# Banded heads of a hybrid attention layer: probabilities turned by DMA transposes instead of TensorE

## The chip, the cores and the metric

The kernel runs on one core of one Trainium2 chip. The metric is the device time of one execution in microseconds. The program has one launch; three runs of the kernel before gave 1187.77, 1191.12 and 1192.73 us, a median of 1191.12.

## What is computed

One decoder layer over 2048 positions of width 1024 (batch 1). A pre-normalised input goes through one projection that feeds two groups of eight heads of 64: the Fox heads (causal attention over all positions with a forget-gate bias) and the banded heads (a sliding window of 128 with a learned sink per head, four query heads to a key head). Each group's output is gated, both go through one output projection, are normalised and added to the input. The change is in the banded heads:

```python
def sliding_window_sink_attention(q, k, v, sinks):
    B, S, _, d = q.shape
    nb = S // Q_BLOCK
    ...
    kk, vv = with_prev(k), with_prev(v)
    s = jnp.einsum('bnqhgd,bnshd->bnhgqs', qb, kk, preferred_element_type=jnp.float32) * (d ** -0.5)
    ...
    band = (rel >= 0) & (rel < WINDOW)
    ...
    s = jnp.where(mask[None, :, None, None], s, -jnp.inf)
    ...
    p = jax.nn.softmax(jnp.concatenate([s, sink], axis=-1), axis=-1)[..., :-1]
    out = jnp.einsum('bnhgqs,bnshd->bnqhgd', p.astype(vv.dtype), vv)
    return out.reshape(B, S, SWA_Q_HEADS * d)
```

A block of 128 queries sees its own block of keys and the one before; the softmax has the sink as one more column.

## The kernel before

**Stages.** The kernel runs its stages one after the other: the start (adaLN, normalised input turned into `hT`), a prologue of projections, the banded stage (about 146 to 431 us of the profile), the Fox stage, and the output projection. Numbers are carried as a high and a low part in fp16, so that a product takes three matmuls (high times high, high times low, low times high).

**Order.** The order within each engine is written out by hand. Projection work is cut into units (3 matmuls of 512 columns, or 12 of 128) in a list `punits`; `fill(n)` issues the next n units, with the weight events that hang on them. `after(n, f)` queues f for the n-th next `tick()`, which is how evacuations of projection results follow some time behind their matmuls. Three PSUM banks `bk` (five in the Fox stage) take the results of projections; an evacuation releases its bank.

**The banded stage.** It works through 32 pairs (`Pair`): a pair is two query heads `j` of one key head and two blocks `i`, `i+1` of 128 queries. That is four score blocks of 128 x 256, or, for the first pair of each `j`, two of 128 x 128 and two of 128 x 256. So a pair has eight blocks of 128 x 128 probabilities (`nt`), and four of the pairs have six. One turn of the loop (L1100) is called a period here. In period n, PE's projection units are issued in four parts with a tick ahead of each, and around them stand:

- `maxima` of pair n (L855): DVE reads the scores from PSUM, adds the band mask, writes them to the tile `sm_` in SBUF, and takes row maxima (L865). POOL puts the sink into the column behind them (L863). One DVE operation makes the four negated maxima `nb` (L869).
- `exps` of pair n after the first part (L871): ACT takes the exponential in place, four operations, with the row sums.
- at the end of the period, `pv` of pair n-1 (L897): PE multiplies the turned probabilities `ptt` with the values (L904); at the next tick DVE scales the result (L910) and POOL sends it to DRAM (L912).
- then `turn` of pair n (L878): PE transposes the f32 probabilities of `sm_` block by block into the PSUM tile `pxb` (L885). At the next tick ACT copies them to fp16 as the high part (L894), and at the tick after that DVE subtracts to get the low part (L890), both into `ptt`. DVE also takes the reciprocal of the row sums there.
- then `scores` of pair n+1 (L844): PE, into the PSUM tile `pss`, of which there is one.
- last, ACT's squares of a piece of the output weights (L1123), and SP's load of the next piece (L1127).

PSUM in this stage: three banks `bk`, two for `pss`, two for `pxb`, one for `pob` (the result of `pv`). Rotated queries come in chunks of 512 positions (`evac_rope`): ACT copies the projection out, SP swaps its halves by four DMAs (L712), DVE forms sine and cosine terms six ticks later, and two ticks after that the chunk's low part is done (L719); the chunk is a tile of the pool `abp` with four buffers. The pool `stp` with two buffers of 2 KB per partition holds the same for the keys, in the prologue only.

**Queues.** SP, POOL and ACT issue DMAs in program order, each waiting where its instruction waits. In the banded stage SP has the four swaps per chunk and one weight load per period; POOL has the weights of later projections, the round trips of their maxima through DRAM (`w_max`, `w_back`), the sink copies and the results.

**Start of the Fox stage.** `key_limbs(hd)` (L1213) makes three limbs of a head's gate sums on DVE, six small operations into the tile `lk`; `key_rows(hd)` (L1225) turns them by a PE matmul (L1199) and has them copied out and sent to the head's tile. Head 1 needs both ahead of the first score step (L1522 to L1525), behind a loop that issues units, maxima of the first head and ticks.

Of the kernel before, what the change touches and what calls it, by code (L numbers as in the profile page):

```python
# [10 lines left out]
F32 = mybir.dt.float32  # L11
F16 = mybir.dt.float16
# [6 lines left out]
P = 128  # L19
# [22 lines left out]
def hybrid_layer(  # L42
# [38 lines left out]
    def sm(n, tag):  # L81
        return small.tile([P, n], F32, tag=tag, name=tag)
# [110 lines left out]
    def after(n, f):  # L193
        late.append([n, f])
# [460 lines left out]
    def open_fox():  # L655
        nonlocal abp
        xlx.close()
        abp = swa_pool("abp", 4)
        early.close()
        fxv = right.enter_context(tc.tile_pool(name="fxv", bufs=1, side="right", reuse_waits="tile"))  # L660
        vt = fx["vt"] = fxv.tile([P, NB, 8, VW], F16, name="vt")
        fx["lk"] = fxv.tile([P, LW], F16, name="lk")
        fx["lq"] = [fxv.tile([P, LW], F16, name=f"lq{n}") for n in range(2)]
        fx["cst"] = cst = fxv.tile([P, XR], F16, name="cst")
        fx["crow"] = fxv.tile([P, P], F16, name="crow")
        for ap, val in ((vt[:, :, :, 64:65], 1.0), (cst[:], 0.0), (fx["lk"][:], 0.0), (fx["lq"][0][:], 0.0),
                        (fx["lq"][1][:], 0.0), (cst[:, 64:65], XA), (cst[:, 65:66], XB),
                        (cst[:, 66:67], XA), (cst[:, 67:68], XB), (cst[:, 68:69], XC)):
            V.memset(ap, val)
# [15 lines left out]
    def swa_pool(name, bufs, **kw):  # L685
        return swa.enter_context(tc.tile_pool(name=name, bufs=bufs, reuse_waits="tile", **kw))
# [147 lines left out]
    class Pair:  # L834
# [20 lines left out]
        def maxima(self):  # L855
            key = f"qb{self.j}"
            snk2 = snk[:, 2 * self.j:2 * self.j + 2]

            self.sm_ = sws.tile([P, 2, 2, 2 * P + 1], F32, tag="ss", name="sm_")
            m = sm(4, "b_m")  # L860
            for e, (i, k0, nk) in enumerate(self.blocks):
                w = nk * P
                G.tensor_copy(self.sm_[:, e, :, w:w + 1], snk2.unsqueeze(2))  # L863
                for h in range(2):
                    V.tensor_tensor_reduce(self.sm_[:, e, h, :w], self.pss[:, h, e * 2 * P:e * 2 * P + w],  # L865
                                           bmask[:, 2 * P - w:], scale=scl[key][:], scalar=snk2[:, h:h + 1],
                                           op0=ALU.add, op1=ALU.max, accum_out=m[:, 2 * e + h:2 * e + h + 1])
            self.nb = sm(4, "b_nb")
            V.tensor_scalar(self.nb[:], m[:], -1.0, LIFT, op0=ALU.mult, op1=ALU.add)  # L869

        def exps(self):  # L871
            self.rs = sm(4, "b_rs")
            for e, (i, k0, nk) in enumerate(self.blocks):
                for h in range(2):
                    p, c = self.sm_[:, e, h, :nk * P + 1], slice(2 * e + h, 2 * e + h + 1)
                    A.activation(p, p, AF.Exp, bias=self.nb[:, c], accum_out=self.rs[:, c])

        def turn(self):  # L878

            nt = self.nt  # L880
            px = ps_t.tile([P, 8, P], F32, tag="t", name="pxb")
            for e, (i, k0, nk) in enumerate(self.blocks):
                for h in range(2):
                    for b in range(nk):
                        PE.transpose(px[:, self.at[e] + h * nk + b, :], self.sm_[:, e, h, b * P:(b + 1) * P], ident[:])  # L885
            self.ptt = ptp.tile([P, 2, 8, P], F16, tag="pt", name="ptb")
            hi, lo = self.ptt[:, 0, 0:nt, :], self.ptt[:, 1, 0:nt, :]

            def low():
                V.tensor_tensor(lo, px[:, 0:nt, :], hi, op=ALU.subtract)  # L890
                self.rinv = sm(4, "b_ri")
                V.reciprocal(self.rinv[:], self.rs[:])

            after(1, lambda: A.activation(hi, px[:, 0:nt, :], AF.Copy))  # L894
            after(2, low)

        def pv(self):  # L897
            j, i = self.j, self.i
# [183 lines left out]
    with swa_order:  # L1082
        fill(N_PRO - 4, tick2)
        psx.close()
        sws = swa_pool("sws", 1)
        ptp = swa_pool("ptp", 1)
        ps_s = swa_pool("ps_s", 1, space=PSUM)
        ps_t = swa_pool("ps_t", 1, space=PSUM)
        ps_pv = swa_pool("ps_pv", 1, space=PSUM)
        wsp = swa_pool("wsp", 2)  # L1090
        wss, wst = sm(16, "a_m"), sm(2, "wst")
        wsq = {}
        base = N_PRO
        NW = len(windows)
        windows[0].scores()
        windows[0].maxima()
        fill(2, tick2)
        windows[0].exps()
        fill(2, tick2)
        for n, wd in enumerate(windows):  # L1100
            goal = base + (N_SWA - base) * (n + 1) // NW
            todo = goal - pos[0]
            part = [todo * (m + 1) // 4 - todo * m // 4 for m in range(4)]
            tick()
            if n:
                wd.maxima()
            fill(part[0])
            tick()
            if n:
                wd.exps()  # L1110
            fill(part[1])
            tick()
            fill(part[2])
            tick()
            fill(part[3])
            if n:
                windows[n - 1].pv()
            wd.turn()
            if n + 1 < NW:
                windows[n + 1].scores()  # L1120

            if n:
                A.activation(wsq[n - 1][:], wsq[n - 1][:], AF.Square, accum_out=wss[:, (n - 1) % 16:(n - 1) % 16 + 1])  # L1123
            if n == 16:
                V.tensor_reduce(wst[:, 0:1], wss[:], axis=AX.X, op=ALU.add)
            wsq[n] = wsp.tile([P, 2 * P], F32, tag="wsq", name="wsq")
            SP.dma_start(wsq[n][:], w_out0[n // 4 * P:(n // 4 + 1) * P, n % 4 * 2 * P:(n % 4 + 1) * 2 * P])  # L1127
        tick()
        fill(5)
        tick()  # L1130
        fill(5)
        tick()
        fill(6)
        windows[NW - 1].pv()
        tick()
        tick()
        A.activation(wsq[NW - 1][:], wsq[NW - 1][:], AF.Square, accum_out=wss[:, 15:16])
        V.tensor_reduce(wst[:, 1:2], wss[:], axis=AX.X, op=ALU.add)
        wsum = sm(1, "w_mx2")
        V.tensor_reduce(wsum[:], wst[:], axis=AX.X, op=ALU.add)  # L1140
# [363 lines left out]
    with tc.manual_schedule():  # L1504
# [8 lines left out]
        pw_ = bk[bank()][:, 0:1]  # L1513
        PE.matmul(pw_, ones[:], wsum[:], start=True, stop=True)
        root_scale(wrt[:], pw_)
        while pos[0] < N_V3 or mi < M_LEAD:
            fill(1)
            if mi < M_LEAD and pos[0] >= N_QK0 - 12:
                munits[mi]()
                mi += 1  # L1520
            tick()
        key_limbs(1)  # L1522
        for _ in range(3):
            tick()
        key_rows(1)  # L1525
# [113 lines left out]
```

## Time and profile before

| | |
|---|---|
| Median of three runs | 1191.12 us |
| Profiled execution: its time, its span | 1192.12 us, 1190.1 us |
| PE, DVE, ACT busy in the span | 96%, 77%, 56% |
| Granted TensorE clock, mean | 0.994 |
| Pairs of the banded stage, blocks turned | 32, of which 28 with eight blocks and 4 with six |

The profile is one execution. A row of a group gives line, engine and operation, out<-in with shapes and count, then busy time and mean ns of one, then the idle time of the engine ahead of them and what ended it. A row of the timeline gives the start in us, the duration, the instruction, and in brackets the idle time before it with its releaser. A row of a window gives the stretch, its length, then busy time (and number of instructions) of PE, PEld (weight loads), DVE, ACT and POOL, the granted clock, the share of the 16 DMA engines, and GB/s. Matmuls overlap each other, so the time that PE is held by a group is read from the start of the group to the start of the next.

### The profile page before, as it was taken

The numbers are of one execution on the slowest core, as the hardware profiler recorded it, in microseconds if no ns is written. First come the engines' busy times: TensorE is split into PE (matmuls) and PEld (weight loads), VectorE is DVE, ScalarE is ACT, GpSimd is POOL, SyncE is SP. The second block draws the span as 40 slices with busy tenths as digits, with TensorE's granted clock in tenths as the row PEclk, the third lists the DMA queues.
The fourth block names the chain that finished last, engine by engine and source line by source line (L and its number), as shares of the span: only waits on it lengthen the run. The fifth ranks groups of instructions, "written<-read, shape, count | busy, mean of one in ns | idle before, by whom it ended". The sixth has DMA issues, their size and how long they took to land.

```text
span 1190.1 us, 27190 instructions
## 1 busy us (share of the span) xinstructions
PE 1146.8 (96%) x10829; PEld 690.1 (58%) x10829; DVE 912.6 (77%) x2261; ACT 665.0 (56%) x1100; POOL 115.2 (10%) x231
## 2 busy tenths in 40 slices
PE   5899999999999998999999999999999999999997
PEld 2465556765568976455555555555555555555553
DVE  7877677777777749588888899887888887766665
ACT  2784346465555511476666666666666778433332
POOL 2000122112222211011000101001000000000000
PEclk9899999999999999999999999999999999999999
DMA  9745443223233332423425332223311345455652
GB/s 331 265 133 90 98 85 89 59 80 90 85 86 72 53 74 53 60 63 87 68 70 81 94 60 63 47 48 77 41 42 41 90 129 174 147 174 181 202 168 90
DMA packets 87579, 120.22 MB, mean 101 GB/s; under 512 B 27508, under 2 KB 63388, under 8 KB 87452
## 3 DMA queue, kind: packets, MB, share of 16 engines
q1 hardware_dynamic: 76184, 85.69, 24.8%
q0 software_dynamic: 10832, 32.50, 13.5%
q8 instruction: 85, 1.39, 0.7%
q14 instruction: 42, 0.34, 0.2%
q10 hardware_dynamic: 436, 0.28, 0.1%
HBM read 71.04 MB, written 25.18 MB: 81 GB/s over the span
## 4 chain that ended last, share of the span: by engine, by line
PE 80%; DVE 10%; DMA 5%; ACT 2%; issue 2%; SPq 1%; DVEq 0%; ACTq 0%
PE bk L314 30%; PE bk L1448 13%; PE bk L332 7%; PE sta L1292 4%; PE sta L1291 4%; PE bk L1242 4%; PE poa L1317 2%; PE poa L1318 2%; PE poa L1315 2%; PE pxb L885 2%; DMA wa<-in_w_ada_dram 2%; PE pss L852 2%; DVE a_m L1245 2%; PE pob L904 2%; DMA sinT<-sn__241 1%
## 5 line engine op out<-in xcount | busy, mean ns | idle before, releaser
L1298 ACT ACTIVATE p<-sta,lift,scl_qk 128x1024 f32<-128x1024 f32 (+2 forms) x160 | 171.9, 1074 | 143.8 <-PE sta L1292 88.0
L314 PE MATMUL bk<-hT,wh_qk 128*128 128x512 f16 x768 | 195.8, 381 | 0.0
L1245 DVE TENSOR_REDUCE a_m<-bk 128x1 f32<-128x512 f32 x192 | 130.3, 685 | 58.1 <-PE bk L1242 56.9
L1448 PE MATMUL bk<-wohl,oz 128*128 128x512 f16 x768 | 172.2, 379 | 0.7 <-DVE oz L1435 0.7
L1305 DVE TENSOR_TENSOR pha<-p,pha 128x1024 f16<-128x1024 f32 (+2 forms) x160 | 169.0, 1057 | 0.2 <-ACT pha L1302 0.2
L1302 ACT ACTIVATE pha<-p 128x1024 f16<-128x1024 f32 (+2 forms) x160 | 148.1, 925 | 8.5 <-PE bk L1242 3.1
L1448 PEld LDWEIGHTS <-oz 128*128 128x128 f16 x768 | 74.2, 99 | 82.3 <-DVE oz L1435 2.8
L314 PEld LDWEIGHTS <-wh_qk 128*128 128x128 f16 x768 | 72.6, 98 | 78.2 <-issue 6.8
L1318 PE MATMUL poa<-vt,pha 128*128 128x65 f16 x1088 | 116.0, 192 | 1.4 <-DVE pha L1305 1.2
L1315 PE MATMUL poa<-vt,pha 128*128 128x65 f16 x1088 | 116.5, 193 | 0.5 <-DVE ona L1324 0.4
L1317 PE MATMUL poa<-vt,pha 128*128 128x64 f16 x1088 | 116.5, 194 | 0.0
L1291 PE MATMUL sta<-T 128*128 128x512 f16 (+1 forms) x320 | 110.9, 346 | 2.4 <-ACT p L1298 2.4
L1242 PE MATMUL bk<-T 66*128 66x512 f16 (+2 forms) x320 | 109.9, 349 | 3.4 <-DVE a_m L1245 3.2
L1315 PEld LDWEIGHTS <-pha 128*128 128x128 f16 x1088 | 101.5, 96 | 15.0 <-DVE ona L1324 1.5
L1292 PE MATMUL sta<-T 69*128 69x512 f16 (+1 forms) x320 | 109.8, 348 | 0.0
L1317 PEld LDWEIGHTS <-pha 128*128 128x128 f16 x1088 | 100.9, 97 | 11.4
L1318 PEld LDWEIGHTS <-pha 128*128 128x128 f16 x1088 | 100.8, 99 | 1.8 <-DVE pha L1305 1.7
L314 PE MATMUL bk<-hT,wh_za 128*128 128x512 f16 x384 | 99.7, 378 | 0.0
L332 PE MATMUL bk<-wh_va,hT 128*128 128x128 f16 x1536 | 90.7, 219 | 0.0
L332 PEld LDWEIGHTS <-hT 128*128 128x128 f16 x1536 | 87.5, 98 | 4.7 <-issue 2.1
L314 PE MATMUL bk<-hT,wh_zb 128*128 128x512 f16 x384 | 89.2, 379 | 0.0
L314 PE MATMUL bk<-hT,wh_qb 128*128 128x512 f16 x384 | 87.4, 379 | 0.0
(490 smaller groups left out, 1846.7 us busy)
## 6 DMA issues: line engine op xcount, KB each, us to landing
hT<-in_x_dram SPq DMA_DIRECT2D x20, 512.0 KB
wa<-in_w_ada_dram SPq DMA_DIRECT2D x16, 512.0 KB
z_d<-tz POOLq DMA_DIRECT2D x32, 256.0 KB, 3.0
T<-stq SPq DMA_DIRECT2D x64, 128.0 KB
T<-o_d SPq DMA_DIRECT2D x16, 512.0 KB
T<-z_d SPq DMA_DIRECT2D x16, 512.0 KB
out_dram<-hT SPq DMA_DIRECT2D x15, 512.0 KB
xt<-in_x_dram SPq DMA_DIRECT2D x12, 512.0 KB
```

Source lines behind the costliest of these rows:

```text
L314: PE.matmul(ps, whl[:, a, k, :], hT[ci][:, b, k, :], start=(k == 0 and n == 0), stop=(k == KT - 1 and n == 2))
L332: PE.matmul(ps[:, u * P:(u + 1) * P], hT[ci][:, a, k, u * P:(u + 1) * P], whl[:, b, k, :], start=(k == 0 and n == 0), stop=(k == KT - 1 an ...
L1242: PE.matmul(mx[:, :w], T[0:XM, 0, i * P:(i + 1) * P], T[0:XM, 2, pc * CH:pc * CH + w], start=True, stop=True)
L1245: V.tensor_reduce(m3[:, u, pc:pc + 1], mx[:, :w], axis=AX.X, op=ALU.max)
L1291: PE.matmul(self.st[:, o:o + w], T[:, 3, kb_], T[:, 1, qc], start=True, stop=False)
L1292: PE.matmul(self.st[:, o:o + w], T[0:XR, 2, kb_], T[0:XR, 0, qc], start=False, stop=not diag)
L1298: A.activation(self.p32[:, :self.w], self.st[:, :self.w], AF.Exp, scale=scl[f"qk{self.hd}"][:], bias=lift[:])
L1305: V.tensor_tensor(self.ph[:, 1, :self.w], self.p32[:, :self.w], self.ph[:, 0, :self.w], op=ALU.subtract)
L1315: PE.matmul(po[:, u, :], ph[:, 0, pq], vt[:, b, hd, 0:65], start=(self.first and n == 0 and u == 0), stop=False)
L1317: PE.matmul(po[:, u, 0:64], ph[:, 0, pq], vt[:, b, hd, 65:VW], start=False, stop=False)
L1318: PE.matmul(po[:, u, :], ph[:, 1, pq], vt[:, b, hd, 0:65], start=False, stop=(self.last and n == len(self.blocks) - 1))
L1448: PE.matmul(py, self.hl[:, i, k, :], w_slot(8 * j + k)[:, cc], start=(k == 0 and m_ == 0), stop=(k == KT - 1 and m_ == 2))
```

## The change

The high and the low part of the probabilities are now made before they are turned. `high` (ACT) writes the fp16 high part of `sm_` to an SBUF tile right behind the exponentials; `low` (DVE) writes the low part to a second tile at the end of the period, with the reciprocal of the row sums. `turn(0)` and `turn(1)` send each of the two tiles through one DMA transpose on SP, which writes the turned blocks into `ptt`: the first after the third part of the projection units, the second at the end of the period. The two tiles are taken from `stp`. PE's transposes and their PSUM tile go; the two banks go to a second score buffer, and the scores of pair n+1 are issued before the fourth part of the units instead of at the period's end. `ptt` gets two buffers for one, `abp` three for four. The offset for the exponentials is made for each query block instead of once for both. At the start of the Fox stage the limbs of head 1 are made within the loop, as soon as the position in the unit list is two short of the end of the value projections, instead of behind the loop.

```diff
@@ open_fox
-        abp = swa_pool("abp", 4)
+        abp = swa_pool("abp", 3)
@@ Pair.maxima
             m = sm(4, "b_m")
+            self.nb = []
             for e, (i, k0, nk) in enumerate(self.blocks):
...
-            self.nb = sm(4, "b_nb")
-            V.tensor_scalar(self.nb[:], m[:], -1.0, LIFT, op0=ALU.mult, op1=ALU.add)
+                nb = sm(2, "b_nb")
+                V.tensor_scalar(nb[:], m[:, 2 * e:2 * e + 2], -1.0, LIFT, op0=ALU.mult, op1=ALU.add)
+                self.nb.append(nb)
@@ Pair.exps
-                    A.activation(p, p, AF.Exp, bias=self.nb[:, c], accum_out=self.rs[:, c])
-
-        def turn(self):
-
-            nt = self.nt
-            px = ps_t.tile([P, 8, P], F32, tag="t", name="pxb")
-            for e, (i, k0, nk) in enumerate(self.blocks):
-                for h in range(2):
-                    for b in range(nk):
-                        PE.transpose(px[:, self.at[e] + h * nk + b, :], self.sm_[:, e, h, b * P:(b + 1) * P], ident[:])
-            self.ptt = ptp.tile([P, 2, 8, P], F16, tag="pt", name="ptb")
-            hi, lo = self.ptt[:, 0, 0:nt, :], self.ptt[:, 1, 0:nt, :]
-
-            def low():
-                V.tensor_tensor(lo, px[:, 0:nt, :], hi, op=ALU.subtract)
-                self.rinv = sm(4, "b_ri")
-                V.reciprocal(self.rinv[:], self.rs[:])
-
-            after(1, lambda: A.activation(hi, px[:, 0:nt, :], AF.Copy))
-            after(2, low)
+                    A.activation(p, p, AF.Exp, bias=self.nb[e][:, h:h + 1], accum_out=self.rs[:, c])
+
+        def parts(self, n):
+
+            same = self.blocks[0][2] == self.blocks[1][2]
+            for es in ([slice(0, 2)] if same else [slice(0, 1), slice(1, 2)]):
+                e, ne = es.start, es.stop - es.start
+                nk = self.blocks[e][2]
+                yield (self.sm_[:, es, :, 0:nk * P], *[
+                    pr[:, self.at[e]:self.at[e] + 2 * ne * nk, :].rearrange("p (e h b) c -> p e h (b c)", e=ne, h=2)
+                    for pr in self.pr[:n + 1]])
+
+        def high(self):
+
+            self.pr = [stp.tile([P, 8, P], F16, tag="st", name="pr") for _ in range(2)]
+            for p32, hi in self.parts(0):
+                A.activation(hi, p32, AF.Copy)
+
+        def low(self):
+            for p32, hi, lo in self.parts(1):
+                V.tensor_tensor(lo, p32, hi, op=ALU.subtract)
+            self.rinv = sm(4, "b_ri")
+            V.reciprocal(self.rinv[:], self.rs[:])
+
+        def turn(self, n):
+
+            if n == 0:
+                self.ptt = ptp.tile([P, 2, 8, P], F16, tag="pt", name="ptb")
+            SP.dma_start_transpose(self.ptt[:, n, 0:self.nt, :], self.pr[n][:, 0:self.nt, :].rearrange("p t c -> p (t c)"))
@@ the loop of the banded stage
-        ptp = swa_pool("ptp", 1)
-        ps_s = swa_pool("ps_s", 1, space=PSUM)
-        ps_t = swa_pool("ps_t", 1, space=PSUM)
+        ptp = swa_pool("ptp", 2)
+        ps_s = swa_pool("ps_s", 2, space=PSUM)
...
             if n:
                 wd.exps()
+            wd.high()
             fill(part[1])
             tick()
             fill(part[2])
             tick()
+            wd.turn(0)
+            if n + 1 < NW:
+                windows[n + 1].scores()
             fill(part[3])
             if n:
                 windows[n - 1].pv()
-            wd.turn()
-            if n + 1 < NW:
-                windows[n + 1].scores()
+            wd.low()
+            wd.turn(1)
@@ start of the Fox stage
+        limbs1 = False
         while pos[0] < N_V3 or mi < M_LEAD:
             fill(1)
             if mi < M_LEAD and pos[0] >= N_QK0 - 12:
                 munits[mi]()
                 mi += 1
+            if pos[0] >= N_V3 - 2 and not limbs1:
+                key_limbs(1)
+                limbs1 = True
             tick()
-        key_limbs(1)
         for _ in range(3):
             tick()
         key_rows(1)
```

## The prediction

> **What bounds the kernel now.** I read the page's busy shares and its chain of waits first, then the banded stage alone, one period of it in order of time, and last the rows that price each moved piece.
>
> ```profile
> span 1190.1 us, 27190 instructions
> PE 1146.8 (96%) x10829; PEld 690.1 (58%) x10829; DVE 912.6 (77%) x2261; ACT 665.0 (56%) x1100; POOL 115.2 (10%) x231
> ...
> PE 80%; DVE 10%; DMA 5%; ACT 2%; issue 2%; SPq 1%; DVEq 0%; ACTq 0%
> ```
> ```profile
> 155.68:410.35 254.67, 254.41 (x2902) 174.00 (x2902) 190.68 (x543) 139.11 (x387) 54.78 (x129) 1.00 0.34 79
> 172.56:181.94 9.38, 9.12 (x75) 5.04 (x75) 9.13 (x27) 3.83 (x12) 1.68 (x5) 1.00 0.37 71
> ```
>
> The first window runs from the scores of pair 1 to those of pair 31: 30 periods of 8.49 us. Its columns are length, then PE, PEld, DVE, ACT and POOL busy, the granted clock, the DMA share. PE is busy 254.41 of 254.67 us at clock 1.00: it waits for nothing, and instructions taken from it shorten the stage. DVE has 6.36 us of work per period, ACT 4.64; the second window is the fullest period for DVE (9.13 of 9.38).
>
> ```profile
> 273.06 0.86 PE L904 MATMUL pob<-vb,ptb 128*128 128x64 f16 x24
> ...
> 273.75 1.07 PE L885 MATMUL pxb<-ident,sm__3722 128*128 128x128 f32 x8
> 273.96 0.42 DVE L910 TENSOR_TENSOR on<-pob,b_ri 128x256 f32<-128x256 f32 x1 [0.82 <-PE pob L904]
> ...
> 274.76 0.83 PE L852 MATMUL pss<-kst,stb 64*128 64x256 f16 x12
> ...
> 275.77 0.54 DVE L865 CUSTOM_DVE_ANT_0 sm__3831<-pss,bmask,snk 128x256 f32<-128x256 f32 x1 [1.39 <-POOL sm__3831 L863]
> ```
> ```profile
> 290.85 0.85 PE L885 MATMUL pxb<-ident,sm__3949 128*128 128x128 f32 x6
> 291.63 0.83 PE L852 MATMUL pss<-kst,stb 64*128 64x256 f16 x12
> ```
>
> This is the end of a period (start, duration, instruction): values of the pair before, eight transposes, scores of the pair after. The transposes hold PE for 274.76 - 273.75 = 1.01 us; for the four pairs with six blocks 291.63 - 290.85 = 0.78.
>
> **The change part by part.** *Transposes off PE:* 28 x 1.01 + 4 x 0.78 = **31.4 us** less PE work, all of it in the stretch without PE idle time.
>
> *High and low part from SBUF instead of PSUM:*
>
> ```profile
> L1305 DVE TENSOR_TENSOR pha<-p,pha 128x1024 f16<-128x1024 f32 x36 | 43.8, 1217 | 0.0
> L890 DVE TENSOR_TENSOR ptb<-pxb,ptb 128x1024 f16<-128x1024 f32 x19 | 23.1, 1216 | 0.0
> L894 ACT ACTIVATE ptb<-pxb 128x1024 f16<-128x1024 f32 x19 | 19.4, 1023 | 23.4 <-PE pxb L885 23.2
> L1302 ACT ACTIVATE pha<-p 128x1024 f16<-128x1024 f32 x38 | 40.1, 1055 | 1.0
> ```
> ```profile
> L869 DVE TENSOR_SCALAR b_nb<-b_m 128x4 f32<-128x4 f32 x31 | 5.5, 177 | 1.1
> ```
>
> The same operations stand in the Fox stage with SBUF sources (L1305, L1302): 1217 against 1216 ns, 1055 against 1023. So nothing on DVE and 0.03 us on ACT per pair. The offset for each half instead of one for both adds one L869 (0.18) per pair. DVE then has 6.36 + 0.18 = 6.54 us of work in a period of 8.49 - 1.01 = 7.48, ACT about 4.7. The fullest period has 9.31 against 9.38 - 1.01 = 8.37: DVE falls 0.9 us behind and catches up in the next, and three result banks lie between it and PE. I cost this at nothing; its cover is that DVE's lag stays under the time PE needs for a bank.
>
> *Two score buffers:* the scores of the next pair go ahead of the last quarter of the period. DVE's wait of 1.39 us ahead of the maxima ends 0.18 us after the scores (274.76 + 0.83), so it goes. Off PE, hence worth nothing by itself, but it gives DVE air. The scores need the rotated queries earlier, by a quarter's matmuls (a fourth of 7.48 less 0.7 for pv and 0.8 for scores, 1.5), pv (0.7) and the transposes (1.0), 3.2 us in all. The tightest of the first chunks, pair 4:
>
> ```profile
> 174.39 0.69 DVE L719 TENSOR_TENSOR stb<-qc,stb 128x512 f16<-128x512 f32 x1
> ...
> 181.94 0.82 PE L852 MATMUL pss<-kst,stb 64*128 64x256 f16 x11
> ```
>
> Ready at 175.08, wanted at 181.94: 6.9 us, of which 3.7 are left. Three query buffers for four: a chunk's slot was read by pairs that lie some three periods back, no wait.
>
> *64 DMA transposes on SP, new, and not in this trace.* Each takes 128 partitions x 1024 fp16 = 262,144 bytes. Nearest rows:
>
> ```profile
> q1 hardware_dynamic: 76184, 85.69, 24.8%
> ...
> z_d<-tz POOLq DMA_DIRECT2D x32, 256.0 KB, 3.0
> ...
> mx_d<-w_mx POOLq DMA_DIRECT2D x23, 0.5 KB, 7.8
> ```
> ```profile
> 155.65 2.42 SPq L712 DMA_DIRECT2D qs<-qf  x4
> 158.11 0.58 SPq L1127 DMA_DIRECT2D wsq<-in_w_out_dram  x1
> ```
>
> Time on the 16 DMA engines, T: SP's queue moved 85.69 MB in 24.8% of 1190.1 us, 290 GB/s while busy, so 0.9 us from below. From above: blocks 128 elements wide have rows of 256 bytes, 1024 of them, 64 per engine; at the queue's mean of 0.248 x 1190.1 x 16 / 76184 = 62 ns per packet, 4.0 us. I take 1.5: the copy with something for short pieces. Two per period are 3.0 beside the present 0.34 x 8.49 = 2.9, in 7.48: room. Issue: 0.60 us of SP each (2.42 / 4), or eight times that, 4.8, if each block is issued by itself. SP has 0.58 + 1.2 us of other issues per period, so I take 0.6. Landing L, from issue to semaphore: 3.0 us for the same bytes from POOL, 7.8 for the slowest small one, plus up to 4.0 of engine time: 3.0 to 11.8. I take 4.
>
> *Who waits.* The first transposing DMA waits for ACT's high part, the second for DVE's low part, now the last DVE work of the period. Behind them on SP stand the rotation copies of L712, used six ticks (one and a half periods) after issue, and the weight load of L1127, used a period later. The low part's DMA has to land before this pair's pv, at the end of the next period. The loop is: pv, output scaling on DVE 0.9 us after pv's start (273.06 to 273.96), a period's DVE work 6.54, L, pv; two periods must hold it: 0.9 + 6.54 + L <= 2 x 7.48, L <= 7.5. At L = 4 there are 3.5 us to spare. The next high part needs the first buffer read out: 7.48 - 1.06 = 6.4 us, enough for 4 as well.
>
> *Key limbs of head 1 earlier:*
>
> ```profile
> 474.49 1.88 DVE L1245 TENSOR_REDUCE a_m<-bk 128x1 f32<-128x512 f32 x3
> ...
> 476.29 0.23 DVE L1216 TENSOR_SCALAR a_cv<-csum,isc_qk 128x16 f32<-128x16 f32 x1
> ...
> 477.38 0.17 DVE L1219 TENSOR_SCALAR lk<-a_cv 128x16 f16<-128x16 f32 x1
> ...
> 477.61 0.25 PE L1199 MATMUL bk<-identh,lk 128*72 128x128 f16 x1 [2.62 <-DVE lk L1219]
> ```
>
> PE waits 2.62 us for six small DVE operations queued behind three reductions. Placed earlier, their 1.26 us (476.29 to 477.55) delay the reductions, for which PE may wait instead: gain 1.4 to 2.6. I take 1.4.
>
> **Sum.** The profiled execution took 1192.12 us (span 1190.1), 1.0 above the median of 1191.12. 1192.1 - 31.4 - 1.4 = 1159.3; less 1.0 for the median, and about 1 us back for first and last pair, where the DMAs' latency has less cover: **1159 us**.
>
> **Rivals.** *B, DVE becomes the bound.* The row at 275.77 names the POOL copy as releaser. If that is true and not the scores, the wait stays: 6.54 + 1.39 = 7.93 per period, gain 0.56 x 31 = 17, time 1191.1 - 17 - 1.4 = 1173. Against it:
>
> ```profile
> 292.61 0.55 DVE L865 CUSTOM_DVE_ANT_0 sm__4069<-pss,bmask,snk 128x256 f32<-128x256 f32 x1 [0.31 <-PE pss L852]
> ...
> 293.31 0.31 POOL L863 COPY sm__4069<-snk 128x2 f32<-128x2 f32 x2
> ```
>
> Here DVE starts 0.7 us ahead of POOL's copy. *C, the landing takes the place of the transposes.* PE waits at pv for the low part if L > 7.5; the period is (7.44 + L) / 2. L = 9 gives 8.22, a gain of 0.27 x 31 = 8 and 1181; even at L = 9.5; 1225 at 11.8. For it: small DMAs landed only after 7.8 us. Against: the one of equal size took 3.0.
>
> *D, slower: the DMA engines become the bound.* If pieces of 256 bytes cost what packets cost, T = 4.0, and a period needs 2 x 4.0 + 2.9 = 10.9 us: 2.4 x 31 = 74 more than before, 1191.1 + 74 - 1.4 = 1264. It decides from T = (8.49 - 2.9) / 2 = 2.8 us.
>
> ```profile
> DMA packets 87579, 120.22 MB, mean 101 GB/s; under 512 B 27508, under 2 KB 63388, under 8 KB 87452
> ```
>
> For it: 27,508 of the packets were under 512 bytes, so the mean of 62 ns is no price of large ones alone. Against: SP's mean packet moved 1.1 KB (85.69 MB / 76184) in those 62 ns, and a quarter of the bytes should cost less.
>
> The Trainium skill (DMA: Bandwidth & Descriptors, Latency and other measured facts) gives DMA transposes 261 GB/s effective, an estimate of 1.0 us for 262,144 bytes. By it the sum is the forecast's, by the packet row it is 1264; no run here shows which.
>
> *E, blocks one after another.* If the eight blocks of a DMA follow each other, each held for at least an issue (0.60), SP is taken for 2 x 4.8 + 1.8 = 11.4 us per period: 2.9 x 31 = 90 more, 1280, and more if a block costs a landing. The loads on SP and POOL in this trace overlap, which speaks against. Beside it stands a rule of the Trainium skill (VectorE: DVE Perf Modes, The three transpose paths): 1309 ns for a 128x128 block through the DMA against 390 on TensorE, with the advice to use TensorE where PSUM will do. Taken block by block that is an estimate of 21 us per period and some 1580 us; no run here shows it.
>
> That the change would not do what it says I give no weight: the PE instructions are gone from the program.
>
> **Chances.** Forecast 0.65 (1154 to 1167 by itself), B 0.10, C 0.08, D 0.12, E 0.05. 0.5% is 6 us; the three runs shown lie 5 us apart, so less can't be told from no change. Faster than 1185: 0.65 + 0.10 + 0.03 of C = 0.78. Within: 0.03 of C, 0.01 of D. Slower: the rest, 0.18. From 1153 (the whole 2.6 for the limbs, nothing given back, and the runs' scatter) to 1200 (C at L = 10, the foot of D) the range holds about 0.8.
>
> **What would show it.** Right: no L885 row, periods near 7.5 us, PE still without idle time there, DVE's wait ahead of L865 gone, no wait at L1199 near the start of the Fox stage. Wrong: PE waiting at L904 for a DMA (C), then a DMA share near 1 (D) or SP's transposes back to back (E); PE waiting for DVE to free banks (B). ACT waiting for its high part's buffer would mean that the first transpose reads out later than 6.4 us.

## The result, and the profile after

| | before | after |
|---|---|---|
| Median | 1190.74 us (1187.77 to 1192.86, 12 runs) | 1197.36 us (1193.61 to 1206.92, 12 runs) |
| Profiled execution: its time, its span | 1192.12 us, 1190.1 us | 1194.08 us, 1192.2 us |

The ratio is 1.0068, 95% interval 1.0044 to 1.0093: the change made the kernel slower by some 7 us, where 1159 us had been forecast. The profiled execution of after is one of its fastest, 3.3 us below the median. Its page:

```profile
span 1192.2 us, 26857 instructions
...
PE 1126.0 (94%) x10581; PEld 663.7 (56%) x10581; DVE 916.2 (77%) x2297; ACT 670.2 (56%) x1104; POOL 115.8 (10%) x231
...
DMA packets 153115, 136.46 MB, mean 114 GB/s; under 512 B 93044, under 2 KB 128924, under 8 KB 152988
...
q1 hardware_dynamic: 141720, 101.95, 35.0%
```

PE lost 248 instructions (10829 to 10581: 28 x 8 and 4 x 6 transposes) and 20.8 us of busy time, and yet the span grew. So it waits somewhere. Next the banded stage as a whole, from the first scores to the end of the last pv, first of before, then of after (length, then PE, PEld, DVE, ACT, POOL busy, granted clock, DMA share, GB/s):

```profile
145.90:431.21 285.31, 285.02 (x3339) 199.18 (x3339) 208.14 (x591) 151.85 (x417) 60.76 (x138) 1.00 0.34 80
```
```profile
144.97:437.22 292.25, 266.28 (x3091) 173.55 (x3091) 211.07 (x626) 156.42 (x421) 61.05 (x138) 0.98 0.76 132
```

Before, PE was idle for 0.3 us of the stage; after, for 292.25 - 266.28 = 26.0, and its mean clock fell to 0.98. The DMA engines are busy for 0.76 of the time, not near 1 (in a short stretch the share can exceed 1, since a packet's whole time counts where it starts). Single periods of after, two quiet ones and the two longest:

```profile
304.50:311.70 7.20, 7.20 (x59) 3.57 (x58) 6.64 (x18) 3.44 (x7) 0.96 (x2) 1.00 0.47 109
311.73:319.00 7.27, 7.27 (x64) 3.73 (x63) 7.13 (x23) 4.38 (x14) 1.63 (x6) 1.00 0.52 124
```
```profile
268.27:279.98 11.71, 8.40 (x68) 4.03 (x68) 7.80 (x22) 5.80 (x18) 2.25 (x6) 1.00 1.31 217
279.98:295.22 15.24, 10.10 (x65) 4.65 (x65) 6.44 (x17) 5.51 (x16) 3.34 (x8) 0.78 0.76 95
```

In the two quiet periods the change does what was forecast: PE works without a gap, in 7.2 and 7.3 us. Of the 31 periods between scores, fifteen last 6.7 to 7.9 us and eight 8.0 to 8.9. The loss sits in eight stretched ones of 9.2 to 15.2 us, which hold 20.0 of PE's 26.0 us of idle time. What PE, ACT and DVE wait for, from the waits of after (total us, times, longest):

```profile
PEld L915 <- DMA ptb<-pr: 28.5, 24, 3.0
ACT pr L894 <- DMA ptb<-pr: 26.2, 10, 5.4
...
PE pob L915 <- DMA ptb<-pr: 23.3, 21, 2.6
...
DVE pr L898 <- DMA ptb<-pr: 15.8, 6, 6.4
```

pv (L915) waits for the transposed tile, and the high and low parts (L894, L898) wait until a transpose has read out their buffer. The transposes themselves are not slow to issue: SP's row for them (ns minimum, median, maximum) is

```profile
L906 SPq DMA_TRANSPOSE ptb<-pr x64: 1211/1248/3419, 150.6 to 426.3; - x64
```

The longest period in order of time (start, duration, instruction, in brackets the wait ahead of it):

```profile
273.70 3.53 SPq L906 DMA_TRANSPOSE ptb<-pr  x2
274.44 0.56 POOL L221 DMA_DIRECT2D mx_d<-w_mx  x1 [5.97 <-DVE w_mx L218]
...
281.97 0.55 POOL L221 DMA_DIRECT2D mx_d<-w_mx  x1 [1.88 <-DVE w_mx L218]
285.18 0.11 PEld L915 LDWEIGHTS <-ptb 128*128 128x128 f16 x2 [2.98 <-DMA ptb<-pr]
285.18 0.23 PE L915 MATMUL pob<-vb,ptb 128*128 128x64 f16 x2 [2.49 <-DMA ptb<-pr]
285.22 1.06 ACT L894 ACTIVATE pr<-sm__3794 128x1024 f16<-128x1024 f32 x1 [5.41 <-DMA ptb<-pr]
...
288.06 1.36 PE L915 MATMUL pob<-vb,ptb 128*128 128x64 f16 x22 [2.65 <-DMA ptb<-pr]
```
```profile
280.00:281.00 1.00, 1.00 (x15) 0.56 (x15) 1.00 (x2) 0.00 (x0) 0.10 (x1) 1.00 0.36 2
...
284.00:285.00 1.00, 0.00 (x0) 0.00 (x0) 0.00 (x0) 0.00 (x0) 0.00 (x0) 1.00 0.71 177
...
286.00:287.00 1.00, 0.00 (x0) 0.00 (x0) 0.00 (x0) 1.00 (x3) 0.04 (x1) 0.74 0.00 0
288.00:289.00 1.00, 0.94 (x18) 0.94 (x19) 0.89 (x1) 0.51 (x2) 0.00 (x0) 0.50 1.27 68
```

The two transposes were issued at 273.70 and 276.00. The trace's single packets show that the last of their data had been written at 277.4 and 278.6, 1.2 us for each; PE was released at 285.18 and 288.06, 7.8 and 9.5 us later. In between, the engines moved 2 GB/s (280 to 281) or nothing (286 to 287) in some stretches. So it is not the data that is late but its signal. What is in flight beside it is L221, the write of a weight matrix's column of maxima to DRAM: `w_max` (L214) sends 128 pieces of 4 bytes, `w_back` (L226) reads them back for all partitions. The DMA rows of this stretch:

```profile
mx_d<-w_mx POOLq DMA_DIRECT2D x2, 0.5 KB, 10.5
```

That is the DMA of "7.8 us" which stood in the prediction. Five of the eight stretched periods lie with such a write (issues near 171.8, 212.7, 274.4, 329.3, 396.3). Of the other three, one has two weight loads of 512 KB in flight (from 268.27), one a read-back L226 (from 343.76, issued at 343.88), and in the one from 242.76 PE waits 1.6 us for weights that ACT and DVE prepare, not for a DMA. The writes issued at 151.9 and 371.0 cost PE next to nothing.

The trace also has the single steps of a signal, which is 16 updates of a semaphore. Those of the write issued at 274.44 come between 282.00 and 284.96. Those of the first transpose come between 282.18 and 285.14, each some 0.2 us behind one of the write's. Those of the second come between 284.72 and 288.02, each 0.1 to 0.2 us ahead of one of L923's write of a result to DRAM (issued at 276.66, 284.92 to 288.16).

The Trainium skill (DMA: Bandwidth & Descriptors, Queues, rings and completion order) says that a semaphore increment lands only after every earlier write of that DMA engine, across its queues. This trace agrees for the first transpose: its data were there at 277.4, and its signal came step by step behind that of a small write that was itself 10.5 us under way. For the second it is open which write held it the three us longer.

### The profile page after: what moved, and what is told of

The parts are those of the page before. It is cut to its first block, busy times and chain, and to the rows that moved or that the text cites. A ratio compares the mean times of both kernels' runs of the same rounds, so it can differ in the third digit from the quotient of the medians.

```text
span 1192.2 us, 26857 instructions
## 1 busy us (share of the span) xinstructions
PE 1126.0 (94%) x10581; PEld 663.7 (56%) x10581; DVE 916.2 (77%) x2297; ACT 670.2 (56%) x1104; POOL 115.8 (10%) x231
## 4 chain that ended last, share of the span: by engine, by line
PE 56%; DVE 8%; issue 6%; DMA 2%; ACT 1%; POOL 1%; DVEq 0%; SPq 0%; POOLq 0%; ACTq 0%
PE bk L314 19%; PE bk L1461 13%; PE sta L1305 4%; PE sta L1304 4%; PE bk L1255 4%; PE poa L1330 2%; PE poa L1331 2%; PE poa L1328 2%; DVE a_m L1258 2%; PE bk L332 1%; DVE pha L1318 1%; PE bk L1420 1%; DMA wsq<-in_w_out_dram 1%; DMA ptb<-pr 1%; PE sta L1307 0%
## 5 line engine op out<-in xcount | busy, mean ns | idle before, releaser
L314 PE MATMUL bk<-hT,wh_qb 128*128 128x512 f16 x384 | 92.5, 389 | 0.0
```

The source lines that it names most:

```text
L314: PE.matmul(ps, whl[:, a, k, :], hT[ci][:, b, k, :], start=(k == 0 and n == 0), stop=(k == KT - 1 and n == 2))
```

## Experiments

Each ratio is against runs of the kernel before that were taken beside it.

**1. The round trip of the maxima left out.** Theory 1 was that the small DRAM writes hold back the transposes' signals.

```diff
-        md = mx_d[len(kaps_seen) % 3]
-        G.dma_start(md[:], mx[:])
-        wq[key].append(md)
+        wq[key].append(mx)
```

`w_back` does nothing then, and each partition uses its own maximum: the maximum over partitions is left out.

> The changed kernel without the round trip of the weight maxima through DRAM (L221 and L226): each partition scales by its own maximum, so the maximum over the partitions is left out; the DVE reduction of the read-back stays, over as many elements. Theory 1 (the transposes' completions are held up behind other DMAs on the same 16 engines, above all behind the 4-byte writes of the maxima, and PE waits at L915 for them): the waits at 180, 222, 285, 288, 338, 406 and 425 us go, some 15 us of PE waits and the slow clock with them, and the time falls from 1197 to 1170-1182. Theory 2 (the DMA engines are short of throughput): 192 KB of small traffic less of some 38 MB, no change, 1195-1199. Theory 3 (the chain low, output scaling, maxima, exponentials, high on DVE and ACT is too long for the new period): no change, apart from POOL no longer being held, 1190-1197.

1170.79 us (1169.44 to 1172.68), ratio 0.981 (0.9796 to 0.9824). Its banded stage:

```profile
144.11:413.30 269.19, 260.39 (x3091) 172.16 (x3091) 211.21 (x626) 155.94 (x421) 49.73 (x118) 0.99 0.67 140
```

292.25 became 269.19: 23 of the stage's lost microseconds belong to the round trip. The same left out of the kernel before:

> The same left out of the kernel before. All theories: nothing on its path waits for these transfers long, so 1188-1191, a ratio of 0.997 to 1.001. If it falls as much as the changed kernel does, the round trip costs by itself and says nothing of the transposes.

1189.44 us, ratio 0.9961 (0.9948 to 0.9974): there it costs 4.6 us, and not in the banded stage, which takes 285.07 us without it. The small writes were in both kernels, but before the change PE waited for no DMA in this stage (0.3 us idle in all).

**2. Is it the write, its read-back, or its size?** From the run without the round trip, one DMA was put back, and its result is read by nobody: once the small write itself, once one of 512 bytes per partition.

```diff
+        G.dma_start(mu_d[len(kaps_seen) % 3][:], mx[:])
...
+        G.dma_start(mu_d[len(kaps_seen) % 3][:], wq[key][0][:, 0, 0:P])
```

> Kernel after without the round trip (the maximum over partitions is left out), but with the write of 4 bytes per partition to DRAM issued as before and never read. Theory 1 (the write itself holds the signals back): 1188 to 1200 us, as the kernel after. Theory 2 (POOL's wait for the write, ahead of the read-back): 1168 to 1175, as the run without the round trip.

> As the unread write, but 512 bytes per partition instead of 4 (128 columns of the weight matrix). If it is the smallness of the pieces that makes the write slow: 1168 to 1177 us. If it is any write of 128 pieces to DRAM: 1185 to 1200.

1205.77 us with the small write (ratio 1.0097, 1.008 to 1.0115) against 1173.47 with 128 times as many bytes (0.9824, 0.9804 to 0.9843). Their banded stages and DMA rows, with the median time to landing, the small write first:

```profile
146.23:446.39 300.16, 269.78 (x3091) 176.50 (x3091) 212.46 (x627) 156.01 (x421) 55.38 (x128) 0.97 0.73 127
```
```profile
143.30:414.46 271.16, 260.68 (x3091) 171.99 (x3091) 211.16 (x626) 155.65 (x421) 55.70 (x129) 0.99 0.69 142
```

```profile
mu_d<-w_mx POOLq DMA_DIRECT2D x23, 0.5 KB, 8.1
```
```profile
mu_d<-wr_va POOLq DMA_DIRECT2D x4, 64.0 KB, 2.6
mu_d<-wr_za POOLq DMA_DIRECT2D x4, 64.0 KB, 3.0
mu_d<-wr_zb POOLq DMA_DIRECT2D x3, 64.0 KB, 3.2
```

POOL waits for neither, since there is no read-back, so theory 2 (POOL's queue) falls. The smallness of the pieces decides, for a write into DRAM. The Trainium skill (DMA: Bandwidth & Descriptors, Specifications) gives 512 bytes as the least size at line rate and says that below it the engine reads, modifies and writes; 8.1 against 2.6 to 3.2 us agrees; but the next experiment's 4-byte pieces, into SBUF, land in 2.0, a difference that this rule does not make.

**3. Small pieces into SBUF.** All of the computation is kept: the 4-byte pieces go into one row of a tile in SBUF, the row goes to DRAM five units of work later as one piece of 512 bytes, and comes back as before.

```diff
-    mx_d = [dram.tile([P, 1], F32, name=f"mx_d{n}") for n in range(3)]
+    mx_d = [dram.tile([1, P], F32, name=f"mx_d{n}") for n in range(3)]
...
-        G.dma_start(md[:], mx[:])
+        row = mxp.tile([P, P], F32, tag="mxr", name="row")
+        G.dma_start(row[0:1, :], mx[:])
...
+    def w_mid(key):
+        md = mx_d[len(kaps_seen) % 3]
+        kaps_seen.append(key)
+        G.dma_start(md[:], wq[key].pop()[0:1, :])
+        wq[key].append(md)
```

> Kernel after with the maxima sent as 4-byte pieces into one row of SBUF, from there to DRAM as one piece of 512 bytes, and read back as before (one more step on POOL's queue). If what holds the signals back is a 4-byte piece written into DRAM: 1170 to 1180 us. If it is any DMA of 4-byte pieces, or POOL's waits for it: 1190 to 1210.

1171.85 us (1169.72 to 1173.82), ratio 0.9816 (0.98 to 0.9831), faster than both kernels. DMA rows, banded stage and PE's wait:

```profile
mxr<-mx_d POOLq DMA_DIRECT2D x23, 64.0 KB, 3.8
...
row<-w_mx POOLq DMA_DIRECT2D x23, 0.5 KB, 2.0
mx_d<-row POOLq DMA_DIRECT2D x23, 0.5 KB, 2.0
```
```profile
144.57:413.72 269.15, 259.49 (x3091) 171.45 (x3091) 211.56 (x626) 155.65 (x421) 65.93 (x148) 1.00 0.70 143
```
```profile
PE pob L920 <- DMA ptb<-pr: 8.3, 10, 1.8
```

The same 128 pieces of 4 bytes land in 2.0 us in SBUF and in 7.9 in DRAM (median of after). How much of this the kernel before gets by itself:

> Kernel before with the maxima through a row of SBUF. The round trip left out of it gave 4.6 us, so between 1187 and 1192 us; below 1180 would mean that the gain of the run with the change is not the change's.

1187.37 us, ratio 0.9954 (0.994 to 0.9968). So with the small writes gone the change is worth 0.9816 / 0.9954 = 0.986, some 16 us; with them it costs 7. The banded stage of this run of before:

```profile
143.22:428.28 285.06, 284.81 (x3339) 199.20 (x3339) 207.67 (x590) 151.71 (x417) 65.84 (x148) 1.00 0.28 78
```

**4. Maxima on TensorE.** For nine matrices of the stage the column is transposed by PE, reduced on DVE and spread by a product with ones; the result stands beside `pob` in one tile (first run) or in a projection bank (second).

```diff
+            PE.transpose(px[0:1, 0:P], mx[:], ident[:])
+            V.tensor_reduce(m1[0:1, :], px[0:1, 0:P], axis=AX.X, op=ALU.max)
...
+            PE.matmul(px[:, P:P + 1], ones[0:1, :], mxr[0:1, :], start=True, stop=True)
+            V.tensor_copy(mx2[:], px[:, P:P + 1])
```

> Kernel after, with the maximum of a weight matrix over the partitions taken by TensorE (a transpose of one column, a maximum on VectorE, a product with ones, in the unused half of the bank of pob) for the nine matrices of the banded stage, in place of the 4-byte writes to DRAM and the read-back. Theory 1 (the small writes hold back the signals of the transposes): 1168 to 1178 us, PE waits for ptb below 20 us in all, against 52 in the kernel after. Theory 2 (the read-back's wait on POOL's queue delays the work behind it): the same, since both go. Theory 3 (the DMA engines or SP's issues are the limit): 1190 to 1200.

> As the run with the maxima on TensorE that took 1189 us, but the column and the product stand in a projection bank taken from the rotation (L177) and not beside pob, so that pv waits for no reader of the maxima and the maxima for no reader of pv. If the loss of that run came from this coupling (pv waiting for the reductions L234 and L251, the transposes of a column for L938): 1170 to 1178 us, with no wait of pv for DVE. If it came from TensorE waiting for VectorE's maxima at all, wherever they stand: 1182 to 1190.

1189.3 us (ratio 0.9959, 0.9945 to 0.9973) and 1186.32 (0.9935, 0.9919 to 0.9951): neither came down to the 1168 to 1178 us hoped for. In the first, PE's waits for the DMA had fallen from 23.3 to 11.2 us (the 52 of its expectation counts the weight loads' waits once more), but pv now waited for DVE's reductions of the neighbouring region, and these for pv's result:

```profile
PE pvb L932 <- DMA ptb<-pr: 11.2, 4, 3.7
...
PE pvb L932 <- DVE w_mx L251: 2.8, 2, 1.9
...
PE pvb L250 <- DVE on L938: 2.2, 2, 1.4
PE pvb L932 <- DVE w_mx L234: 2.0, 1, 2.0
```

In the second that coupling is gone, and the time is still in the band given for "TensorE waiting for VectorE at all". A small write near 400 us stayed in it, outside the part that was changed. One period of 11.45 us is stretched by the edit itself: PE waits 1.63 us at the product with ones (L250) until DVE has emptied the bank, and its clock is half from 167.1 to 170.6. In all, 13.7 us of this stage ran at half clock, against none with the SBUF row. So this says only that the SBUF row is the better way, not how much a wait for DVE costs by itself.

**5. Unread transposes in the kernel before.** Two DMA transposes per period of some other data were added, whose results nobody reads.

```diff
+        def idle_turn():
+            tdst = tdp.tile([P, 8, P], F16, tag="td", name="tdst")
+            SP.dma_start_transpose(tdst[:], vb[:, 0:4].rearrange("p t h c -> p (t h c)"))
```

> The kernel before, with its PE transposes, and two DMA transposes of 128 x 1024 fp16 per period beside them that nobody reads (source: the value tile, destination: a tile of their own; query buffers 3 instead of 4). Theory 1 and theory 3: the load alone harms nobody, since nothing on PE's path waits for a DMA; 1189-1194. Theory 2: the weight loads and swaps come late and PE waits for them; over 1197.

1238.99 us, ratio 1.0367 (1.0344 to 1.039): by the expectation, the DMA engines would be short of throughput. The waits point elsewhere. ACT waited for the load of `wsq`, which stands behind them on SP:

```profile
ACT wsq L1131 <- DMA wsq<-in_w_out_dram: 132.4, 31, 12.0
```

So that load was put at the top of the period, ahead of the transposes, which were moved apart:

> Kernel before with two unread transposes per period, as in the run that took 1239 us, but the load of wsq ahead of them, at the top of the period, and the two a period's three quarters apart, so that SP does not wait with the second for the first. Theory of the queue (the 48 us came from SP, whose load of wsq stood behind a waiting transpose): 1188 to 1200 us. Theory of the engines (the transposes take the DMA engines' time from everything else): above 1225.

1233.29 us, ratio 1.0324 (1.0297 to 1.0351), in the band given for the engines: the theory of the queue's order falls. The wait went to the next DMA behind, the rotation copies, and SP itself waits up to 9.1 us for its transposes' tile:

```profile
DVE qs L725 <- DMA qs<-qf: 33.5, 8, 7.7
```
```profile
SPq L1095 <- DMA tdst<-vb: 144.3, 53, 9.1
```

The same kernel without the round trip (the maximum over partitions is left out):

> Kernel before with the two unread transposes per period placed as in the run that took 1233 us (load of wsq first), without the round trip of the maxima (the maximum over partitions is left out). If the 39 us of that run came from the small writes holding up the transposes and what stands behind them on SP: 1189 to 1200 us. If the transposes cost it by themselves (engines, SP's issue): above 1215.

1188.75 us (1188.62 to 1188.89), ratio 0.9958 (0.9945 to 0.9971), the same as before without the round trip and without transposes (1189.44). Its banded stage:

```profile
143.80:428.87 285.07, 284.81 (x3339) 199.22 (x3339) 207.68 (x590) 151.62 (x417) 49.73 (x118) 1.00 0.65 135
```

Sixty-four transposes at a DMA share of 0.65 cost nothing by themselves; together with the small writes they cost 39 us or more, though nobody reads them. So throughput was not the reason for the 1239 and 1233 us either, and rivals D and E of the prediction fall with this.

**6. What is left after the small writes.** In the run with the SBUF row PE is still idle for 269.15 - 259.49 = 9.7 us, 8.3 of them for a transposed tile and 1.0 for weights that ACT and DVE prepare. Four edits were tried on it: weight loads of 512 KB cut into four DMAs; the load of `wsq` ahead of the transposes; both; and pv a quarter of a period later, for more slack.

```diff
+        raw, o, ks = wq[key][0], 0, slice(2 * m, 2 * m + 2)
...
+            G.dma_start(raw[:, ks, o:o + n], w_in0[:, col0:col0 + n].rearrange("(k p) n -> p k n", p=P)[:, ks])
...
+            if n > 1:
+                windows[n - 2].pv()
...
-            if n:
-                windows[n - 1].pv()
```

The cut load runs for `m` from 0 to 3, two units of work apart, so that its last quarter is issued six units after the first.

> The run with the maxima through a row of SBUF (1171.9 us), and each weight load of the banded stage cut from 512 KB into four DMAs of 128 KB, two units of work apart. If the landings are now late because of the large loads: 1165 to 1169 us. If because of all traffic together (loads, z, o, rotation copies, transposes): 1170 to 1173.

> The same run (1171.9 us), with the load of wsq at the top of the period, ahead of the transposes on SP's queue, uncut weight loads. If ScalarE's wait for wsq at the end of a period delays the exponentials and high parts of the next and by them the transposes: 1166 to 1170 us. If it lies beside other work: 1170 to 1173.

> Both edits, cut weight loads and early wsq. If the two causes add: 1161 to 1167 us; 1170 to 1173 if neither is one.

> The run with the maxima through a row of SBUF (1171.9 us), with the values of a pair (pv) moved from the end of the next period to the end of the first quarter of the one after, some 2 us later, so that a transposed tile may land 2 us later before TensorE waits. If the 9.7 us that TensorE is idle in the stage come from too little slack at pv: 1162 to 1167 us, and pv's waits for ptb below 3 us. If the late landings hold up ScalarE and VectorE through the two pr tiles just as much: 1169 to 1173.

The runs of before beside these differ (medians of 1193.54 for the first row, 1193.41 for the last, 1192.28 for the rest), so the ratios compare.

| | median us | ratio (interval) |
|---|---|---|
| SBUF row alone | 1171.85 | 0.9816 (0.98 to 0.9831) |
| loads cut | 1183.61 | 0.992 (0.9903 to 0.9937) |
| wsq early | 1171.97 | 0.9829 (0.981 to 0.9848) |
| both | 1180.91 | 0.99 (0.9883 to 0.9916) |
| pv later | 1170.15 | 0.9801 (0.9789 to 0.9814) |

Cutting the loads makes it worse: PE's waits for `ptb` rose from 8.3 us in 10 waits to

```profile
PE pob L931 <- DMA ptb<-pr: 13.8, 13, 2.1
```

That does not show that more DMAs in flight cost more than large ones, since the cut also ends each load later. DVE, which takes the maxima of a matrix in between the low parts, then waits for the load, 22.3 us in nine waits against 1.4 in one without the cut:

```profile
DVE w_mx L229 <- DMA wr_va<-in_w_in_dram: 7.1, 4, 4.0
DVE w_mx L229 <- DMA wr_qb<-in_w_in_dram: 6.9, 2, 5.0
```

Which of the two it is was not tested. The same cut on the run with a projection bank:

> The run with the maxima in a projection bank, and each load of a weight matrix of the banded stage cut from one DMA of 512 KB into four of 128 KB, two units of work apart. If the large loads, above all the two at once near 265 us, hold the signals back as the small writes do: 3 to 8 us below the run without the cut. If they only take the engines' time: no difference beyond 1.5 us.

1184.12 us, ratio 0.9923 (0.9907 to 0.994), against 0.9935 (0.9919 to 0.9951) without it: no difference to be told.

The early `wsq` does nothing. The later pv takes PE's waits for `ptb` down to 3.2 us and yet the time hardly moves. ACT waits longer for the two `pr` tiles, and PE for weights that ACT and DVE prepare, 6.1 us against 1.0; PE's idle time in the stage is 9.3 us:

```profile
ACT pr L899 <- DMA ptb<-pr: 12.0, 8, 3.0
```
```profile
PE bk L319 <- ACT wh_zb L257: 3.7, 1, 3.7
PE pob L920 <- DMA ptb<-pr: 3.2, 4, 1.3
```

With the SBUF row alone, ACT's wait for `pr` was 6.6 us in 5 waits. The same slack on the changed kernel itself:

> The changed kernel itself with values moved in the same way, small pieces to DRAM as they were. If 2 us more of slack at pv carry it over the 7 to 10 us that a small write takes: below 1180 us. If not, because the holds are longer than that and reach the high and low parts through the two pr tiles: 1186 to 1196.

1198.86 us, ratio 1.0059 (1.0037 to 1.008), as without it, and above both bands:

```profile
ACT pr L894 <- DMA ptb<-pr: 39.4, 12, 7.3
...
PE pob L915 <- DMA ptb<-pr: 12.5, 11, 4.3
```

PE's waits for the DMA halve, and ACT's grow from 26.2 to 39.4 us. A hold of 8 to 10 us passes through whichever of the two stages has less slack. More `pr` and `ptt` tiles were not tried.

**7. Key limbs alone.**

```diff
+            if pos[0] >= N_V3 - 2 and not limbs1:
+                key_limbs(1)
+                limbs1 = True
```

> The kernel before with the limbs of head 1 made within the loop, the last part of the change alone. By the prediction 1.4 to 2.6 us less: 1188.1 to 1189.3 beside 1190.7, and the 2.6 us wait at the key rows' matmul gone. If the reductions behind it are delayed by as much: no change.

1192.07 us against 1193.97 of before, ratio 0.9986 (0.9976 to 0.9996): 1.7 us, by the interval 0.5 to 2.9. PE's waits for `lk`, before and with the limbs earlier:

```profile
PE bk L1199 <- DVE lk L1219: 3.4, 3, 2.6
```
```profile
PE bk L1199 <- DVE lk L1219: 0.8, 2, 0.5
```

As the prediction allowed, PE waits for the delayed reductions instead: there, its wait for `a_m` rose from 0.4 to 1.6 us.

## Why the prediction was wrong

*The step that failed is the landing L.* The prediction bounded it by "3.0 us for the same bytes from POOL, 7.8 for the slowest small one", as a property of the new DMA, took one value of 4, and gave rival C 0.08 with "Against: the one of equal size took 3.0". Both rows were right at once. By the last of a transpose's 16 updates, known for 61 of the 64 in after, L has a median of 4.5 us, close to the 4, but runs from 2.8 to 12.0. Eight lie over the limit of 7.5 that the loop had: six of these were issued close to a 4-byte write of the 7.8 us row, two beside weight loads of 512 KB. With the SBUF row the median is 3.8 and the longest 6.7. So the 7.8 was not the worst case of something similar but another DMA's time that the transposes' signals took over. The stage's mean period, (412.0 - 152.2) / 30 = 8.66 us by the starts of the scores, is what C's formula gives for L = 9.9 in every period. In fact it is not one value: quiet periods run at 7.2 to 7.8 us, and a few are stretched to 15. So that 1197 us lies close to the 1200 which the prediction gave for C at L = 10 is luck.

The limit was too wide as well. With the SBUF row no L exceeds 6.7, and PE still waits 8.3 us for the tile. The loop counted DVE's work without a gap; in that run DVE's low part waits for ACT's high part, which no term of the loop has:

```profile
DVE pr L903 <- ACT pr L899: 13.7, 12, 4.7
```

That this wait uses up the slack is likely, but no run isolates it.

How the stage came to 292.25 us, where 285.31 - 31.4 = 253.9 and part of the 1 us given back had been forecast, from the stage rows of after, of the run with the SBUF row, and of before (the three parts make 38.7, of which 0.3 us of idle time stood in before as well):

- *Small writes, 23.1 us* (292.25 - 269.15). Of them 26.0 - 9.7 = 16.3 are PE waiting, and 266.28 - 259.49 = 6.8 are the same instructions counted longer. In after, 8.6 us of PE's work fell into stretches at half clock (180.7 to 184.1 and 286.5 to 293.3), some 4.3 us of these; with the SBUF row the clock was whole throughout the stage. The clock stood in no term of the sum.
- *Other waits, 9.7 us* of PE idle time once the small writes are gone, 8.3 of them for a transposed tile. The place of `wsq` is not the cause. The size of the weight loads is not settled, and nothing else was isolated.
- *Transposes off PE, 5.9 us less than forecast:* 31.4 was taken from the start of the transposes to that of the scores; PE's busy time in the stage fell by 285.02 - 259.49 = 25.5. From the start of each instruction to that of the next, the transposes did hold PE for 31.1 us in before. But each of the 31 projection matmuls that now stand right ahead of the scores holds PE some 96 ns longer than one ahead of its like, 3.0 us in all (before, the last transpose had this time, 205 ns against 114). Another 2.3 us are matmuls right ahead of a wait, whose modelled end the profile counts as work.

By the medians the small writes weigh more than in the one profiled execution: 1.0068 against 0.9816 is some 30 us, where the two spans differ by 24.3. Outside the stage the profiled span fell by 4.8 us instead of 1.4; the limbs are 1.7 of these, the rest was not traced.

Point by point, the rest: *T* was about right: the two transposes at 276 us moved their data in 1.2 us each, and two unread ones per period fit with room, share 0.65. That also is far from E's eight blocks one after another. *Issue* was twice what was taken, 1.25 us against 0.6, and cost nothing: the last run of unread transposes shows that SP has the time. *High and low part, offsets:* DVE rose by 2.9 us over the stage, ACT by 4.6; PE's waits for DVE in the stage are 0.7 us, so B did not come. *Two score buffers:* DVE's waits of 1.39 us ahead of the maxima are gone from the waits of after. *Key limbs:* 1.7 us, within the 1.4 to 2.6. *"ACT waiting for its high part's buffer"* and *"PE waiting at L904 for a DMA"* were named as signs of the prediction being wrong, and both came (L894 and L915 of after).

## What to carry to other kernels

Before work is moved from an engine to a DMA whose signal the critical engine waits for, list every other DMA that is in flight in that stage and look first at the smallest: a long landing time of some other DMA is not its private matter. If there are writes of a few bytes per piece into DRAM, gather them into one row in SBUF first (2.0 + 2.0 us in place of 7.9 here); that edit turned this change from 7 us slower into 22 us faster than before (5 of them its own). Slack for late signals is worth only what the tightest buffer in the loop has of it.

## What the runs showed of the hardware that was not expected

- 128 pieces of 4 bytes took 7.9 us to land in DRAM (median; 6.8 to 10.5), 2.0 in SBUF (median; 1.9 to 4.8); one piece of 512 bytes took 2.0 into DRAM, 128 pieces of 512 bytes 2.6 to 3.2 (medians).
- While such a write is under way, signals of other DMAs come late even when their data are long written (7.8 and 9.5 us in the case above), and in parts of that time the engines move next to nothing.
- Waits of 2 to 3 us can cost twice, because the granted clock falls. It was half from 180.7, after 3.4 us in which PE was busy for 1.1 us and its longest wait was 2.09; and half from 286.5, after 3.4 us with 0.23 of work. The Trainium skill (TensorE: Matmul & The Clock Gate, Part 1) has the clock go to half after an idle window of about 3.4 us. The second case agrees but for the 0.23 us of work; in the first, less idle time was enough.
- Four loads in place of one of 512 KB, two units of work apart, raised the kernel's time by 12 us beside the transposes (1183.61 against 1171.85); whether by their number or by their later end is open.
